# The HGRN head pipeline of a fused two-block layer, written out in another instruction order

## The chip, the cores and the metric

One core of a Trainium2 chip runs the whole kernel: TensorE (PE), VectorE (DVE), ScalarE (ACT), GpSimd (POOL) and SyncE (SP), which issues the loads. The metric is the device time of one execution, in microseconds. A head, below, is one of the eight heads of the HGRN recurrence.

## The reference, cut to what matters

The kernel computes two transformer-like blocks on 512 tokens of width 1024 with a context of 256 tokens. The change concerns one branch of the first block, the HGRN2 recurrence in both directions over 8 heads of 128 x 128, with the context scanned first:

```python
def _hgrn_gates(f_pre, lb):
    logf = jnp.log(lb + (1.0 - lb) * jax.nn.sigmoid(fp))
    k = (1.0 - lb) * jax.nn.sigmoid(-fp)

def body(S, inp):                       # _hgrn_scan, one chunk
    qc, kc, vc, lf = inp
    b = jnp.cumsum(lf, axis=2)
    decay = jnp.exp(jnp.where(mask, diff, -jnp.inf))
    attn = jnp.einsum('bhtd,bhtsd,bhsd->bhts', qc, decay, kc)
    o = jnp.einsum('bhtd,bhdv->bhtv', qc * jnp.exp(b), S) + jnp.einsum('bhts,bhsv->bhtv', attn, vc)
    S_new = jnp.exp(b_last)[..., None] * S + jnp.einsum(...)
    return S_new, o

hcf, s_f = scan_fn(*ctx_fwd, init)      # _bidir_scan: context, then latent, both directions
hlf, _ = scan_fn(*lat_fwd, s_f)
hcb, s_b = scan_fn(*_flip_t(ctx_bwd), init)
hlb, _ = scan_fn(*_flip_t(lat_bwd), s_b)
return hcf + jnp.flip(hcb, axis=2), hlf + jnp.flip(hlb, axis=2)
```

q is `silu` of a projection, f and k come from one projection for each direction, and v from another. All are float32.

## The kernel before, in words

Features lie on the 128 partitions and tokens along the free side. Every weight block is loaded by SP into `wraw` (3 buffers) and split into a rounded part `whi` on ACT (L203) and a remainder `wlo` on DVE (L204); `mm3` then multiplies `whi` by the two parts of the input (L215, L216) and `wlo` by the first (L218). A projection of 512 tokens is 24 such matmuls.

The recurrence is done without a scan over chunks: blocks of 8 tokens get running products of the gates (`hgrn_gates`, DVE, with two small ACT copies, L854 and L859 for direction 0, L865 and L870 for direction 1), block products are doubled level by level up to 128 tokens (`hgrn_blocks`, L898 and L913), and the attention matrix is put together from products at five sizes: `hgrn_level` makes `QM` on DVE and `KM` on POOL (L953, L956) and multiplies them into the PSUM banks X and Z (L961); the products inside a block of 8 go to Y1 and Y2 (L997). ACT copies X to `at` (L1035), DVE merges Z, Y1 and Y2 in with masks (L1036 to L1039), POOL adds the diagonal (L1040). `hgrn_ctx` makes the decays E of the context (DVE L882, L887, L890; POOL L891); E and the decayed keys `KL` (L1007) are transposed on PE (L1017, L1021), copied to `kt` by ACT (L1018, L1022) and multiplied with v into the state products `pk` (L1048, L1050). The states `st` start with an ACT copy (L1052) and go on in six DVE updates (L1063). The output is three matmuls for each 128 tokens (L1068 to L1070), read by ACT (L1075, L1076).

`hgrn_pipe` runs this as a software pipeline: in round h it finishes head h and prepares head n = h + 1 (projections, gates, block products, q). It stands in `tc.manual_schedule` (in `block1_hgrn`) for PE, DVE, ACT and POOL: these four engines issue the stage's instructions in the order in which the code writes them, and instructions of the next stage may be put between them. The loads of SP are placed by the planner. Buffers that set waits: PSUM `a` 4 banks (X, Z, Y1, Y2 and both `pk`), `p` 2 (all projections), `t` 2 (transposes and output); in SBUF `whi`, `wlo`, `wraw` 3 each and `w2` 17, which holds F, K, the q sigmoid, q, Q1, QM, KM, QL, KL, `at` and `st`.

In the order before, round h writes: gate projection 0 with its F and K sigmoids; q; levels 3 and 2; Y1, Y2; gate projection 1 with its sigmoids; levels 1 and 0; QL, KL; gates 0; all transposes with their `kt` copies; both context projections; the first weight split of head n + 1; gates 1; the `at` copy and the masks; block products; state products; both context decays; q projection; second weight split; state updates; output products; third split.

Of the kernel before, what the change touches and what calls it, by code (L numbers as in the profile page):

```python
# [8 lines left out]
F32 = mybir.dt.float32  # L9
F32R = mybir.dt.float32r  # L10
# [132 lines left out]
class Net:  # L143
# [668 lines left out]
    def hgrn_fx(self, h, d, wt):  # L812

        nc = self.nc
        j, c = (self.HFF, self.HFB)[d] + h, d * 8 + h
        ps = self.proj(wt, "x")
        F, K = self.w2("F"), self.w2("K")
        for t, b, sc in ((F, self.v("b_mix"), 1.0), (K, self.nbm, -1.0)):
            nc.scalar.activation(t.rearrange("p w r -> p r w"), ps.rearrange("p (r w) -> p r w", r=8), AF.Sigmoid,
                                 bias=b[:, j : j + 1], scale=sc)  # L820
            if t is F:
                nc.scalar.activation(F, F, AF.Identity, scale=self.omlb[:, c : c + 1], bias=self.lb[:, c : c + 1])
        return F, K

# [10 lines left out]

    def hgrn_gates(self, h, d, F, K, PS0):

# [15 lines left out]
        if d == 0:  # L853
            nc.scalar.activation(at(k_ + 2, q_ + 4), f(3, 4), AF.Copy)  # L854
            mu(at(k_ + 1, q_ + 5), f(2, 4), f(3, 5))
            mu(at(k_ + 0, q_ + 6), at(k_ + 1, q_ + 5), f(1, 6))
            mu(one(q_ + 7), one(q_ + 6), f(7))
            mu(PS0[:, 0, d], one(k_ + 0), f(0))
            nc.scalar.activation(PS0[:, 1, d], one(q_ + 7), AF.Copy)  # L859
            nc.vector.reciprocal(at(q_ + 0, k_ + 7), at(k_ + 0, q_ + 7))  # L860
            mu(at(q_ + 1, k_ + 6), at(q_ + 0, k_ + 7), f(1, 7))
            mu(at(q_ + 2, k_ + 5), at(q_ + 1, k_ + 6), f(2, 6))
            mu(one(k_ + 4), one(k_ + 5), f(5))
        else:
            nc.scalar.activation(at(q_ + 3, k_ + 5), f(3, 4), AF.Copy)  # L865
            mu(at(q_ + 2, k_ + 6), f(2, 4), f(3, 5))
# [8 lines left out]
        K1 = hx[:, 4 + 2 * (h % 2) + d].rearrange("p (b e) -> p b e", e=8)  # L875
        nc.gpsimd.tensor_tensor(K1, K, C[:, 1].rearrange("p (b e) -> p b e", e=8), ALU.mult)
        return K1

# [41 lines left out]
    def hgrn_q(self, h, ps):  # L920

        nc = self.nc
        bq = self.v("b_mix")[:, self.HQ + h : self.HQ + h + 1]
        sg, q = self.w2("sg"), self.w2("q")
        p8 = ps.rearrange("p (r w) -> p r w", r=8)
        nc.scalar.activation(sg.rearrange("p w r -> p r w"), p8, AF.Sigmoid, bias=bq)
        return sg, q, bq, p8

    def hgrn_q1(self, h, sg, q, bq, p8):
        nc = self.nc  # L930
        pm = lambda t: t.rearrange("p w r -> p r w")
# [9 lines left out]

    def hgrn_level(self, lv, dst, hb, Q1, K1, lev):

# [5 lines left out]
        for (o, a, p, i, e) in ((QM, Q1[0], pv(0, 0), 1, nc.vector), (QM, Q1[1], pv(1, 1), 0, nc.vector),  # L949
# [7 lines left out]
        qm, km = QM.rearrange("p b e -> p (b e)"), KM.rearrange("p b e -> p (b e)")  # L957
        for c in range(4):
            for b in range(128 // hb):
                bs = slice(c * 128 + b * hb, c * 128 + b * hb + hb)  # L960
                nc.tensor.matmul(dst[b * hb : b * hb + hb, bs], km[:, bs], qm[:, bs], start=True, stop=True)  # L961

    def hgrn_pipe(self, v):
# [9 lines left out]
        raw = self.hgrn_w(0)  # L973
        wt = [self.hgrn_split(r) for r in raw]
        PS0, K1, E = ps0(), [], []
        for d in range(2):
            K1.append(self.hgrn_gates(0, d, *self.hgrn_fx(0, d, wt[d]), PS0))
# [5 lines left out]
        wt = [self.hgrn_split(r) for r in raw]  # L983
        for h in range(8):
            n = h + 1
            more = n < 8
            if more:
                fx = [self.hgrn_fx(n, 0, wt[0])]
                PS0, K1n = ps0(), []
            Q1 = self.hgrn_q1(h, *pq)  # L990
            X, Z, Y1, Y2 = [self.bank("a") for _ in range(4)]
            self.hgrn_level(3, X, 128, Q1, K1, lev)
            self.hgrn_level(2, X, 64, Q1, K1, lev)
            for Y, d in ((Y1, 0), (Y2, 1)):
                for c in range(4):
# [14 lines left out]
            if more:  # L1010
                K1n.append(self.hgrn_gates(n, 0, *fx[0], PS0))
            kts = []
            for d in range(2):
                kt = w.tile([128, 5, 128], F32, tag="w5", bufs=2, name=self.nm("kt"))
                pt = self.bank("t")
                for i in range(2):
                    nc.tensor.transpose(pt[:, i * 128 : i * 128 + 128], E[d][:, i * 128 : i * 128 + 128], self.ident)  # L1017
                nc.scalar.activation(kt[:, 0:2], pt[:, :256].rearrange("p (c t) -> p c t", c=2), AF.Copy)  # L1018
                pt = self.bank("t")
                for i, c in enumerate(orders[d]):  # L1020
                    nc.tensor.transpose(pt[:, i * 128 : i * 128 + 128], KE[d][:, c * 128 : c * 128 + 128], self.ident)  # L1021
                nc.scalar.activation(kt[:, 2:5], pt[:, :384].rearrange("p (c t) -> p c t", c=3), AF.Copy)  # L1022
                kts.append(kt)
# [12 lines left out]
            nc.vector.copy_predicated(v4(at), m4(self.m8), v4(Z))  # L1036
# [28 lines left out]
            po = self.bank("o", [128, 4, 128])  # L1065
            for c in range(4):
# [1114 lines left out]
```

## Time and profile before

| | us |
|---|---|
| median of 3 runs | 2699.94 (2699.52 to 2700.64) |
| profiled execution, device time | 2698.25 |
| its span | 2696.5 |
| the HGRN heads, first to last output products | about 775 to 1103 |
| PE busy over the span | 2540.4 (94%) |
| DVE, ACT, POOL busy | 1592.2 (59%), 997.0 (37%), 461.4 (17%) |

How to read it: the span is the stretch between the first and the last instruction of one profiled execution; shares over all of it mix stages with different limits, so the rows further below are cut to single heads. In a timeline a row gives its start, how long it lasted, the engine, the line and what it wrote and read; neighbours of one kind are merged (`x4`), and a bracket tells how long the engine was idle before it and which instruction's end released it.

### The profile page before, as it was taken

The numbers are of one execution on the slowest core, as the hardware profiler recorded it, in microseconds if no ns is written. First come the engines' busy times: TensorE is split into PE (matmuls) and PEld (weight loads), VectorE is DVE, ScalarE is ACT, GpSimd is POOL, SyncE is SP. The second block draws the span as 40 slices with busy tenths as digits, with TensorE's granted clock in tenths as the row PEclk, the third lists the DMA queues.
The fourth block names the chain that finished last, engine by engine and source line by source line (L and its number), as shares of the span: only waits on it lengthen the run. The fifth ranks groups of instructions, "written<-read, shape, count | busy, mean of one in ns | idle before, by whom it ended". The sixth has DMA issues, their size and how long they took to land. (4 is left out here: it accounts for less than half of the span.)

```text
span 2696.5 us, 37860 instructions
## 1 busy us (share of the span) xinstructions
PE 2540.4 (94%) x15116; PEld 2177.0 (81%) x15116; DVE 1592.2 (59%) x2855; ACT 997.0 (37%) x1760; POOL 461.4 (17%) x539
## 2 busy tenths in 40 slices
PE   6999999999977877999999999999999998999998
PEld 4888888898866766889888898888886667988887
DVE  8777767746546546433543365666564676666665
ACT  6312212235333333242532244232343466533333
POOL 3000000021223323421400011034012351100001
PEclk8999999999988888999999999999999998999999
DMA  6535556512100101111133343344414223323332
GB/s 224 179 111 186 211 188 220 203 39 95 59 24 32 40 24 40 57 29 53 55 123 96 94 128 100 94 137 155 130 63 145 57 64 96 110 93 99 100 99 71
DMA packets 88305, 277.92 MB, mean 103 GB/s; under 512 B 12912, under 2 KB 31104, under 8 KB 79936
## 3 DMA queue, kind: packets, MB, share of 16 engines
q1 hardware_dynamic: 85344, 265.00, 30.4%
q0 software_dynamic: 2064, 7.35, 0.8%
q10 hardware_dynamic: 720, 3.15, 0.3%
q8 instruction: 119, 1.95, 0.3%
q14 instruction: 58, 0.48, 0.1%
HBM read 262.88 MB, written 12.59 MB: 102 GB/s over the span
## 5 line engine op out<-in xcount | busy, mean ns | idle before, releaser
L204 DVE TENSOR_TENSOR wlo<-wraw,whi 128x1024 fp32r<-128x1024 f32 (+1 forms) x341 | 424.9, 1252 | 288.5 <-ACT whi L203 159.4
L203 ACT ACTIVATE whi<-wraw 128x1024 fp32r<-128x1024 f32 (+1 forms) x341 | 354.1, 1052 | 492.3 <-PE psa L216 157.8
L215 PE MATMUL psp<-xmh,whi 128*128 128x512 f32 (+1 forms) x760 | 280.6, 378 | 3.2 <-ACT whi L203 2.1
L216 PE MATMUL psp<-xml,whi 128*128 128x512 f32 (+1 forms) x744 | 270.8, 372 | 0.0
L350 POOL TENSOR_TENSOR ssum<-ssum,sq 128x256 f32<-128x256 f32 x40 | 30.2, 755 | 962.0 <-ACT sq L348 961.7
L215 PE MATMUL psa<-xmh,whi 128*128 128x512 f32 x496 | 193.8, 391 | 0.0
L216 PE MATMUL psa<-xml,whi 128*128 128x512 f32 x496 | 193.7, 390 | 0.0
L215 PE MATMUL psu<-xmh,whi 128*128 128x512 f32 x496 | 193.5, 390 | 0.0
L216 PE MATMUL psu<-xml,whi 128*128 128x512 f32 x496 | 193.3, 390 | 0.0
L215 PE MATMUL pso<-hh,whi 128*128 128x512 f32 (+1 forms) x512 | 183.5, 364 | 3.4 <-DVE hr L496 3.4
L216 PE MATMUL pso<-hl,whi 128*128 128x512 f32 (+1 forms) x512 | 183.5, 364 | 0.0
L305 DVE SCALAR_TENSOR_TENSOR ajunk<-araw,crow 128x1024 bf16<-128x1024 f32 x128 | 156.2, 1221 | 26.1 <-DMA araw<-in_ada_r_dram 19.1
L215 PEld LDWEIGHTS psp<-xmh,whi 128*128 128x128 f32 x760 | 147.4, 194 | 28.7 <-ACT whi L203 2.6
L218 PE MATMUL psp<-xmh,wlo 128*128 128x512 f32 (+1 forms) x744 | 170.1, 368 | 0.0
L216 PEld LDWEIGHTS psp<-xml,whi 128*128 128x128 f32 x744 | 143.6, 193 | 23.0 <-issue 0.6
L492 DVE SCALAR_TENSOR_TENSOR xr<-pso,hgate,xr 128x512 f32<-128x512 f32 x128 | 95.2, 748 | 107.8 <-PE pso L218 107.6
L218 PEld LDWEIGHTS psp<-xmh,wlo 128*128 128x128 f32 x744 | 129.3, 189 | 26.1 <-issue 4.4
L218 PE MATMUL pso<-hh,wlo 128*128 128x512 f32 (+1 forms) x512 | 144.5, 363 | 0.0
L218 PE MATMUL psa<-xmh,wlo 128*128 128x512 f32 x496 | 126.8, 389 | 0.0
L218 PE MATMUL psu<-xmh,wlo 128*128 128x512 f32 x496 | 124.0, 390 | 0.0
L215 PEld LDWEIGHTS pso<-hh,whi 128*128 128x128 f32 x512 | 96.7, 189 | 18.0 <-DVE hr L496 3.6
L444 ACT ACTIVATE hh<-sa 128x512 fp32r<-128x512 f32 x66 | 36.7, 560 | 197.3 <-DVE sa L441 197.3
(661 smaller groups left out, 5804.6 us busy)
## 6 DMA issues: line engine op xcount, KB each, us to landing
araw<-in_ada_r_dram SPq DMA_DIRECT2D x52, 1024.0 KB, 5.3
wraw<-in_ffn_in_dram SPq DMA_DIRECT2D x88, 512.0 KB, 4.2
wraw<-in_mix_fm_dram SPq DMA_DIRECT2D x65, 512.0 KB, 3.6
wraw<-in_ffn_out_dram SPq DMA_DIRECT2D x44, 512.0 KB, 3.7
wraw<-in_up_dram SPq DMA_DIRECT2D x44, 512.0 KB, 3.7
wraw<-in_down_dram SPq DMA_DIRECT2D x22, 512.0 KB, 3.7
araw<-in_ada_w_dram SPq DMA_DIRECT2D x8, 1024.0 KB, 11.7
wraw<-in_mix_out_dram SPq DMA_DIRECT2D x14, 512.0 KB, 3.7
```

The costliest lines, as they stand in the source:

```text
L203: nc.scalar.activation(hi, raw, AF.Copy)
L204: nc.vector.tensor_tensor(lo, raw, hi.bitcast(F32), ALU.subtract)
L215: self.nc.tensor.matmul(ps, wh, xh, start=k == 0, stop=False)
L216: self.nc.tensor.matmul(ps, *((wl, xh) if last else (wh, xl)), start=False, stop=False)
L218: self.nc.tensor.matmul(ps, *((wh, xl) if last else (wl, xh)), start=False, stop=k == n - 1)
L305: nc.vector.scalar_tensor_tensor(junk, w[:, h], 1.0, cr[:, n], ALU.mult, ALU.mult, accum_out=o[:, k : k + 1])
L350: (eng or nc.vector).tensor_tensor(acc, acc, t, ALU.add)
L444: nc.scalar.activation(hh, sa, AF.Copy)
L492: self.anchor = nc.vector.scalar_tensor_tensor(res[n], p, gt[:, n : n + 1], res[n], ALU.mult, ALU.add)
```

## The change

The same instructions are written in another order, and four helpers are cut in two so that their parts can stand apart: the weight split (`hgrn_hi` on ACT, `hgrn_lo` on DVE), the gate sigmoids (F in `hgrn_fx`, K in `hgrn_kx`), the gates (`hgrn_gates` becomes a generator that stops behind its first ACT copy, with K1 in `hgrn_k1`) and the levels (`hgrn_level` for the elementwise part, `hgrn_products` for the matmuls). The transposes of one direction with their copies become `hgrn_turn`. q is written over its own sigmoid, so one `w2` buffer less is taken.

Round h now writes: q of head h; gate projection 0, F, the copy L854, K; levels 3 and 2 with their products; Y1, Y2; the elementwise part of levels 1 and 0; QL, KL; the remainder of the q weights of head n; the rest of gates 0 and K1; both context decays of head h; gate projection 1, F, the copy L865; the products of levels 1 and 0; the `at` copy; the transposes and copies of direction 0; the rest of gates 1, K, K1; context projection 0; the transposes and copies of direction 1; the loads of head n + 1 and the first `whi`; the masks; context projection 1; the first `wlo`; the state products; the second `whi`; block products; state updates; the second `wlo`; q projection; the third `whi`; output products. Ahead of the loop the first weight split of head 1 goes before the q projection of head 0. The diff, cut to its core (line numbers of the old file):

```diff
@@ -802 +802 @@
-    def hgrn_split(self, raw):
-        h, l = self.split_w(raw, [KT, 128])
+    def hgrn_hi(self, raw):
+        t = [self.wp.tile([128, KT, 128], F32R, tag="w" + i, name=self.nm("w" + i)) for i in ("hi", "lo")]
+        self.nc.scalar.activation(t[0], raw, AF.Copy)
+        return t, raw
+
+    def hgrn_lo(self, x):
+        (h, l), raw = x
+        self.nc.vector.tensor_tensor(l, raw, h.bitcast(F32), ALU.subtract)
         return [(h[:, k], l[:, k]) for k in range(KT)]
...
@@ -852 +863 @@ def hgrn_gates
             nc.scalar.activation(at(k_ + 2, q_ + 4), f(3, 4), AF.Copy)
+            yield
             mu(at(k_ + 1, q_ + 5), f(2, 4), f(3, 5))
...
@@ -921 +937 @@ def hgrn_q, hgrn_q1
-        sg, q = self.w2("sg"), self.w2("q")
+        sg = self.w2("sg")
...
-        nc = self.nc
+        nc, q = self.nc, sg
...
@@ -970 +999 @@ def hgrn_pipe
         fc = [self.hgrn_fc(0, d, wt[d]) for d in range(2)]
+        raw = self.hgrn_w(1)
+        wt[0] = self.hgrn_lo(self.hgrn_hi(raw[0]))
         pq = self.hgrn_q(0, self.proj(wt[2], "x"))
         lev, ends = self.hgrn_blocks(PS0)
-        E = [self.hgrn_ctx(0, d, *fc[d]) for d in range(2)]
-        raw = self.hgrn_w(1)
-        wt = [self.hgrn_split(r) for r in raw]
+        wt[1] = self.hgrn_lo(self.hgrn_hi(raw[1]))
+        wq = self.hgrn_hi(raw[2])
         for h in range(8):
             n = h + 1
-            more = n < 8
+            more, last = n < 8, n >= 7
+            Q1 = self.hgrn_q1(h, *pq)
             if more:
-                fx = [self.hgrn_fx(n, 0, wt[0])]
                 PS0, K1n = ps0(), []
-            Q1 = self.hgrn_q1(h, *pq)
+                F, ps = self.hgrn_fx(n, 0, wt[0])
+                gates = self.hgrn_gates(n, 0, F, PS0)
+                next(gates)
+                K = self.hgrn_kx(n, 0, ps)
             X, Z, Y1, Y2 = [self.bank("a") for _ in range(4)]
-            self.hgrn_level(3, X, 128, Q1, K1, lev)
-            self.hgrn_level(2, X, 64, Q1, K1, lev)
+            for lv, hb in ((3, 128), (2, 64)):
+                self.hgrn_products(X, hb, *self.hgrn_level(lv, Q1, K1, lev))
...
-            if more:
-                fx.append(self.hgrn_fx(n, 1, wt[1]))
-            self.hgrn_level(1, X, 32, Q1, K1, lev)
-            self.hgrn_level(0, Z, 128, Q1, K1, lev)
+            low = [(X, 32, *self.hgrn_level(1, Q1, K1, lev)), (Z, 128, *self.hgrn_level(0, Q1, K1, lev))]
...
             if more:
-                K1n.append(self.hgrn_gates(n, 0, *fx[0], PS0))
...
+                wt[2] = self.hgrn_lo(wq)
+                next(gates)
+                K1n.append(self.hgrn_k1(n, 0, K))
+            E = [self.hgrn_ctx(h, d, *fc[d]) for d in range(2)]
             if more:
-                fc = [self.hgrn_fc(n, d, wt[d]) for d in range(2)]
-                wq = wt[2]
-            if n < 7:
+                F, ps = self.hgrn_fx(n, 1, wt[1])
+                gates = self.hgrn_gates(n, 1, F, PS0)
+                next(gates)
+            for x in low:
+                self.hgrn_products(*x)
+            at = flat(self.w2("at"))
+            nc.scalar.activation(at, X, AF.Copy)
+            kts = [self.hgrn_turn(E[0], KE[0], orders[0])]
+            if more:
+                next(gates)
+                K = self.hgrn_kx(n, 1, ps)
+                K1n.append(self.hgrn_k1(n, 1, K))
+                fc = [self.hgrn_fc(n, 0, wt[0])]
+            kts.append(self.hgrn_turn(E[1], KE[1], orders[1]))
+            if not last:
                 raw = self.hgrn_w(n + 1)
-                wt = [self.hgrn_split(raw[0])]
-            if more:
-                K1n.append(self.hgrn_gates(n, 1, *fx[1], PS0))
-            at = flat(self.w2("at"))
+                hi = self.hgrn_hi(raw[0])
...
-            nc.scalar.activation(at, X, AF.Copy)
             nc.vector.copy_predicated(v4(at), m4(self.m8), v4(Z))
...
             nc.gpsimd.tensor_tensor(at, at, self.dg, ALU.add)
-            T128 = ends
             if more:
-                lev, ends = self.hgrn_blocks(PS0)
+                fc.append(self.hgrn_fc(n, 1, wt[1]))
+            if not last:
+                wt[0] = self.hgrn_lo(hi)
             pks, S = [], []
...
+            if not last:
+                hi = self.hgrn_hi(raw[1])
+            T128 = ends
             if more:
-                E = [self.hgrn_ctx(n, d, *fc[d]) for d in range(2)]
-                pq = self.hgrn_q(n, self.proj(wq, "x"))
-            if n < 7:
-                wt.append(self.hgrn_split(raw[1]))
+                lev, ends = self.hgrn_blocks(PS0)
             for i in range(3):
...
+            if not last:
+                wt[1] = self.hgrn_lo(hi)
+            if more:
+                pq = self.hgrn_q(n, self.proj(wt[2], "x"))
+            if not last:
+                wq = self.hgrn_hi(raw[2])
             po = self.bank("o", [128, 4, 128])
...
-            if n < 7:
-                wt.append(self.hgrn_split(raw[2]))
```

## Rows read from the trace of the kernel before

**Rows 1.** The page's first line, span of the profiled execution.

```profile
span 2696.5 us, 37860 instructions
```

**Rows 2.** Windows: us, busy PE, PEld, DVE, ACT, POOL; PEclk, DMA, GB/s.

```profile
877.31:928.45 51.14, 38.82 (x254) 34.32 (x254) 26.65 (x60) 17.24 (x34) 16.42 (x18) 0.87 0.10 30
...
1110.00:1300.00 190.00, 188.67 (x1311) 164.37 (x1309) 65.55 (x157) 69.47 (x219) 51.28 (x69) 1.00 0.14 44
```

**Rows 3.** Timeline, PE, head 3: start us, us, instruction, [idle before <-releaser].

```profile
887.97 1.67 PE L961 MATMUL psa<-QM,KM 128*128 128x128 f32 x24
889.57 2.05 PE L997 MATMUL psa<-Q,hgx 128*128 128x128 f32 x16
891.38 0.48 PE L215 MATMUL psp<-xmh,whi 128*128 128x512 f32 x1
...
897.01 1.55 PE L961 MATMUL psa<-QM,KM 128*32 128x32 f32 x40
...
901.84 0.44 PE L1017 MATMUL pst<-ident,E 128*128 128x128 f32 x2 [2.74 <-ACT kt L1018]
...
902.58 0.36 PE L215 MATMUL psp<-xmh,whi 128*128 128x256 f32 x1
...
913.64 1.22 PE L1048 MATMUL psa<-v,kt 128*128 128x128 f32 x4 [5.06 <-ACT at L1035]
...
917.81 0.48 PE L215 MATMUL psp<-xmh,whi 128*128 128x512 f32 x1
...
923.35 0.39 PE L1068 MATMUL pso<-v,at 128*128 128x128 f32 x2
...
928.45 0.80 PE L1070 MATMUL pso<-st,QL 128*128 128x128 f32 x2 [4.49 <-DVE st L1063]
```

**Rows 4.** Timeline, PE, head 6.

```profile
1065.04 1.22 PE L1048 MATMUL psa<-v,kt 128*128 128x128 f32 x4 [2.89 <-ACT at L1035]
```

**Rows 5.** Timeline, ACT, head 3.

```profile
897.12 1.18 ACT L819 ACTIVATE F<-psp,vec 128x512 f32<-128x512 f32 x1 [5.76 <-PE psp L218]
898.33 0.81 ACT L822 ACTIVATE F<-F,lbc,omlb 128x512 f32<-128x512 f32 x1
...
900.00 0.43 ACT L854 ACTIVATE hgx<-F 128x128 f32<-128x128 f32 x1
...
901.42 0.37 ACT L1018 ACTIVATE kt<-pst 128x256 f32<-128x256 f32 x1
...
913.00 0.58 ACT L1035 ACTIVATE at<-psa 128x512 f32<-128x512 f32 x1
...
923.55 1.19 ACT L926 ACTIVATE sg<-psp,vec 128x512 f32<-128x512 f32 x1 [5.19 <-PE psp L218]
```

**Rows 6.** Timeline, DVE, head 3.

```profile
878.38 1.17 DVE L932 SCALAR_TENSOR_TENSOR q<-psp,vec,sg 128x512 f32<-128x512 f32 x1
...
883.59 1.28 DVE L1006 TENSOR_TENSOR QL<-Q,ps 128x512 f32<-128x512 f32 x2
...
912.05 0.70 DVE L852 TENSOR_TENSOR hgx<-hgx,F 128x128 f32<-128x128 f32 x2
...
915.17 0.72 DVE L1036 COPY_PREDICATED at<-m,psa 128x512 f32<-128x512 int32 x1
...
917.94 0.28 DVE L898 TENSOR_TENSOR tots<-ps 128x128 f32<-128x128 f32 x1
...
921.72 0.41 DVE L882 TENSOR_SCALAR fc<-fc,omlb,lbc 128x256 f32<-128x256 f32 x1
...
925.62 1.23 DVE L204 TENSOR_TENSOR wlo<-wraw,whi 128x1024 fp32r<-128x1024 f32 x1 [1.33 <-ACT whi L203]
926.76 1.63 DVE L1063 SCALAR_TENSOR_TENSOR st<-st,tots,psa 128x128 f32<-128x128 f32 x6
```

**Rows 7.** Timeline, POOL, head 3.

```profile
881.66 4.33 POOL L956 TENSOR_TENSOR KM<-hgx,ps 128x256 f32<-128x256 f32 x2 [4.29 <-DVE QM L956]
```

**Rows 8.** Timeline, DVE, head 7.

```profile
1081.55 5.23 DVE L956 TENSOR_TENSOR QM<-Q,ps 128x256 f32<-128x256 f32 x6
```

More of the change, by code (lines that the diff above doesn't have):

```diff
@@ L814, in hgrn_fx, with hgrn_sig, hgrn_kx @@
         nc = self.nc
-        j, c = (self.HFF, self.HFB)[d] + h, d * 8 + h
+        c = d * 8 + h
         ps = self.proj(wt, "x")
[L817 to L823, printed above, removed]
+        F = self.hgrn_sig(h, d, ps, self.v("b_mix"), 1.0)
+        nc.scalar.activation(F, F, AF.Identity, scale=self.omlb[:, c : c + 1], bias=self.lb[:, c : c + 1])
+        return F, ps
+    def hgrn_sig(self, h, d, ps, b, sc):
+        t, j = self.w2("F"), (self.HFF, self.HFB)[d] + h
+        self.nc.scalar.activation(t.rearrange("p w r -> p r w"), ps.rearrange("p (r w) -> p r w", r=8), AF.Sigmoid,
+                                  bias=b[:, j : j + 1], scale=sc)
+        return t
+    def hgrn_kx(self, h, d, ps):
+        return self.hgrn_sig(h, d, ps, self.nbm, -1.0)
     def hgrn_fc(self, h, d, wt):
@@ L834, in hgrn_fc, with hgrn_gates @@
         return out
-    def hgrn_gates(self, h, d, F, K, PS0):
+    def hgrn_gates(self, h, d, F, PS0):
         nc, hx = self.nc, self.hgx
@@ L865, in hgrn_gates @@
             nc.scalar.activation(at(q_ + 3, k_ + 5), f(3, 4), AF.Copy)
+            yield
             mu(at(q_ + 2, k_ + 6), f(2, 4), f(3, 5))
@@ L874, in hgrn_gates, with hgrn_k1 @@
             mu(one(k_ + 3), one(k_ + 2), f(2))
-        K1 = hx[:, 4 + 2 * (h % 2) + d].rearrange("p (b e) -> p b e", e=8)
-        nc.gpsimd.tensor_tensor(K1, K, C[:, 1].rearrange("p (b e) -> p b e", e=8), ALU.mult)
+        yield
+    def hgrn_k1(self, h, d, K):
+        K1 = self.hgx[:, 4 + 2 * (h % 2) + d].rearrange("p (b e) -> p b e", e=8)
+        self.nc.gpsimd.tensor_tensor(K1, K, self.hgx[:, 2 * d + 1].rearrange("p (b e) -> p b e", e=8), ALU.mult)
         return K1
@@ L940, in hgrn_q1, with hgrn_level @@
         return out
-    def hgrn_level(self, lv, dst, hb, Q1, K1, lev):
+    def hgrn_level(self, lv, Q1, K1, lev):
         nc = self.nc
@@ L956, in hgrn_level, with hgrn_products @@
                 e.tensor_tensor(bv(o)[:, :, i], bv(a)[:, :, i], x.unsqueeze(3).broadcast_to([128, 32 // m, m, 8]), ALU.mult)
-        qm, km = QM.rearrange("p b e -> p (b e)"), KM.rearrange("p b e -> p (b e)")
+        return QM.rearrange("p b e -> p (b e)"), KM.rearrange("p b e -> p (b e)")
+    def hgrn_products(self, dst, hb, qm, km):
         for c in range(4):
@@ L960, in hgrn_level, with hgrn_turn @@
                 bs = slice(c * 128 + b * hb, c * 128 + b * hb + hb)
-                nc.tensor.matmul(dst[b * hb : b * hb + hb, bs], km[:, bs], qm[:, bs], start=True, stop=True)
+                self.nc.tensor.matmul(dst[b * hb : b * hb + hb, bs], km[:, bs], qm[:, bs], start=True, stop=True)
+    def hgrn_turn(self, E, KE, order):
+        nc = self.nc
+        kt = self.wk.tile([128, 5, 128], F32, tag="w5", bufs=2, name=self.nm("kt"))
+        for n, src, cs in ((0, E, (0, 1)), (2, KE, order)):
+            pt = self.bank("t")
+            for i, c in enumerate(cs):
+                nc.tensor.transpose(pt[:, i * 128 : i * 128 + 128], src[:, c * 128 : c * 128 + 128], self.ident)
+            nc.scalar.activation(kt[:, n : n + len(cs)], pt[:, : 128 * len(cs)].rearrange("p (c t) -> p c t", c=len(cs)), AF.Copy)
+        return kt
     def hgrn_pipe(self, v):
@@ L972, in hgrn_pipe @@
                 nc.gpsimd.memset(self.hgx[:, 2 * d + i].rearrange("p (b e) -> p b e", e=8)[:, :, e : e + 1], 1.0)
-        raw = self.hgrn_w(0)
-        wt = [self.hgrn_split(r) for r in raw]
-        PS0, K1, E = ps0(), [], []
+        wt = [self.hgrn_lo(self.hgrn_hi(r)) for r in self.hgrn_w(0)]
+        PS0, K1 = ps0(), []
         for d in range(2):
-            K1.append(self.hgrn_gates(0, d, *self.hgrn_fx(0, d, wt[d]), PS0))
+            F, ps = self.hgrn_fx(0, d, wt[d])
+            K = self.hgrn_kx(0, d, ps)
+            for _ in self.hgrn_gates(0, d, F, PS0):
+                pass
+            K1.append(self.hgrn_k1(0, d, K))
         fc = [self.hgrn_fc(0, d, wt[d]) for d in range(2)]
+        raw = self.hgrn_w(1)
+        wt[0] = self.hgrn_lo(self.hgrn_hi(raw[0]))
         pq = self.hgrn_q(0, self.proj(wt[2], "x"))
         lev, ends = self.hgrn_blocks(PS0)
-        E = [self.hgrn_ctx(0, d, *fc[d]) for d in range(2)]
-        raw = self.hgrn_w(1)
-        wt = [self.hgrn_split(r) for r in raw]
+        wt[1] = self.hgrn_lo(self.hgrn_hi(raw[1]))
+        wq = self.hgrn_hi(raw[2])
         for h in range(8):
             n = h + 1
-            more = n < 8
+            more, last = n < 8, n >= 7
+            Q1 = self.hgrn_q1(h, *pq)
             if more:
-                fx = [self.hgrn_fx(n, 0, wt[0])]
                 PS0, K1n = ps0(), []
-            Q1 = self.hgrn_q1(h, *pq)
+                F, ps = self.hgrn_fx(n, 0, wt[0])
+                gates = self.hgrn_gates(n, 0, F, PS0)
+                next(gates)
+                K = self.hgrn_kx(n, 0, ps)
             X, Z, Y1, Y2 = [self.bank("a") for _ in range(4)]
-            self.hgrn_level(3, X, 128, Q1, K1, lev)
-            self.hgrn_level(2, X, 64, Q1, K1, lev)
+            for lv, hb in ((3, 128), (2, 64)):
+                self.hgrn_products(X, hb, *self.hgrn_level(lv, Q1, K1, lev))
             for Y, d in ((Y1, 0), (Y2, 1)):
@@ L1010, in hgrn_pipe @@
             if more:
-                K1n.append(self.hgrn_gates(n, 0, *fx[0], PS0))
[L1012 to L1023, printed above, removed]
-            if more:
-                fc = [self.hgrn_fc(n, d, wt[d]) for d in range(2)]
-                wq = wt[2]
-            if n < 7:
+                wt[2] = self.hgrn_lo(wq)
+                next(gates)
+                K1n.append(self.hgrn_k1(n, 0, K))
+            E = [self.hgrn_ctx(h, d, *fc[d]) for d in range(2)]
+            if more:
+                F, ps = self.hgrn_fx(n, 1, wt[1])
[13 more added lines that the diff above has]
+            if not last:
                 raw = self.hgrn_w(n + 1)
-                wt = [self.hgrn_split(raw[0])]
-            if more:
-                K1n.append(self.hgrn_gates(n, 1, *fx[1], PS0))
-            at = flat(self.w2("at"))
+                hi = self.hgrn_hi(raw[0])
             m4 = lambda m: m.unsqueeze(1).broadcast_to([128, 4, 128])
             v4 = lambda t: t.rearrange("p (c t) -> p c t", c=4)
-            nc.scalar.activation(at, X, AF.Copy)
             nc.vector.copy_predicated(v4(at), m4(self.m8), v4(Z))
```

4 lines of the change are left out of this document (2 added, 2 removed).

## The prediction

> **What bounds the kernel now.** The change touches one stage only, the HGRN recurrence, so I first cut the span into stages with the windows view. From one head's output products to the next head's takes 51.14 us, and in it TensorE (PE) is busy 38.82 us at a mean granted clock of 0.87; right after the stage, from 1110 to 1300 us, it is busy 188.67 of 190 us at a clock of 1.00 [rows 2]. Nothing else is near full inside a head: VectorE 26.65 us, ScalarE 17.24, GpSimd 16.42. So the stage is bound by a ring of waits, and what follows it is bound by PE and takes over whatever time the stage gives back.
>
> Second I read PE's own timeline of head 3 for its waits. There are three: 2.74 us before the second set of transposes, for a `kt` copy of ScalarE; 5.06 us before the state products, for the `at` copy of ScalarE; 4.49 us before the output products, for VectorE's state update `st` [rows 3]. Together 12.29 us. Heads 0 to 5 repeat these three; head 6 has the first and 2.89 us of the second, and not the third [rows 4], since projections of the next stage fill in there; head 7 has little.
>
> Third, the same timeline shows the clock. The state products behind the 5.06 us wait, 20 instructions, take 913.64 to 917.81, 4.17 us, while 16 instructions of the same shape on `Q,hgx` take 1.81 us (889.57 to 891.38), 0.113 each [rows 3]: 1.2 against 2.4 GHz. After the 2.74 us wait nothing slows. So a long wait is paid a second time behind it.
>
> PE's work for one head at full clock, by starts in rows 3: X and Y products 3.41 (887.97 to 891.38), the two gate projections 5.63 each (891.38 to 897.01), low-level products and first transposes 2.09 (897.01 to 901.84 less 2.74), second transposes 0.74, two context projections 6.00 (902.58 to 913.64 less 5.06), q projection 5.54, state products 20 x 0.113 = 2.26, output products 24 x 0.113 = 2.71. Sum 34.0 us. The head's 51.14 is then 34.0 of work, 12.29 of waits, and 4.84 of low clock (1.91 of it on the state products).
>
> **The change, part by part.** No arithmetic instruction is added or dropped; the same ones stand in another order on the four written-out queues. I measure time from T, the end of the projection for the next head's backward gates (897.01 in rows 3).
>
> *First wait.* In the kernel before, `kt` stands on ScalarE behind both sigmoids of d=1 and the gate copy L854 of d=0, which starts at 900.00; `kt` runs at 901.42 though the transposes ended at 899.10 [rows 3, 5]. L854 held VectorE's gates up too. In the change L854 comes right behind F of d=0, before the second projection; `at` and the first `kt` come right behind L865. PE goes from the first transposes to a context projection, whose bank was freed long before, so `kt` has 3.0 us of cover. The wait goes.
>
> *Second wait.* The `at` copy ran at 913.00, behind the weight copies and all gate work of d=1 [rows 5]. Now its turn is at T + 2.56: F starts with the end of the projection (897.12), its scaling ends at 899.14, which is T + 2.13, and L865 takes 0.43 [rows 5]. PE wants the bank at T + 2.09 + 3.0 + 0.74 + 3.0 = T + 8.8. The wait goes with its low clock. The second state bank is Z's and needs VectorE's first mask copy, below.
>
> *Third wait.* S waited at 926.76 for the block products (917.94 to 921.72), the context decays from 921.72 and a weight remainder at 925.62 [rows 6]. Now the decays stand before F of d=1 and the second remainder after S. VectorE's new run from T: second gate product at T + 2.56; gates 3.12 (912.05 to 915.17) plus at most 0.8, because L870 now stands behind `at` (0.58) and two `kt` copies (0.37 and at most 0.58) where it would be wanted 0.70 in: T + 6.5. Masks 2.77 (915.17 to 917.94): T + 9.3. Weight remainder 1.23: T + 10.5. Blocks 3.78: T + 14.3. S 1.63: T + 15.9 [rows 5, 6]. PE reaches the output products at T + 8.8 + 2.26 + 5.54 = T + 16.6. So S is 0.7 us early: this is the tightest place of the new order, and the wait goes only just.
>
> *Closing the ring.* The q sigmoid runs T + 16.6 to 17.8 (1.19). q to QL takes 6.49 on VectorE when GpSimd is not in the way (878.38 to 884.87): T + 24.3; the moved remainder of the q weights 1.23: T + 25.5 [rows 5, 6]. PE has outputs until 19.3 and the next gate projection until 25.0, F is ready at 27.1, L854 at 27.5. Gates until 31.2 (0.5 more for L859, which waits behind the K sigmoid), decays at most 3.9 (921.72 to 925.62): T + 35.1. The next d=1 gates can start at 34.0 + 2.56 = T + 36.6. So VectorE is free 1.5 us early and the ring closes on PE's 34.0.
>
> *New waits on in-order queues.* L859 on ScalarE waits for VectorE's gates with F of d=1 queued behind it; it is due near T + 28.5, F at T + 34.0. L870 has the K sigmoid of d=1 behind it, and the second context projection needs the bank which that sigmoid frees: sigmoid done at about T + 5.6, PE there at T + 5.8. Covered by 0.2 us; if VectorE starts these gates x late, PE loses about x here. On GpSimd the K1 product of d=0 now stands ahead of the decay products; the first is wanted by the transposes at T + 35.4 and ready by about T + 33.3. The three weight loads of SP move behind the second transposes; two of their buffers are free a whole head early, the third by the moved remainder at T + 25.5 with some 26 us until ScalarE wants it. The hi copies run after `kt`, after `st` and after the q sigmoid, each behind the last reader of its buffer. I put all of these at nothing. Writing q over its sigmoid and taking K's buffer later frees buffers of the 17; no row prices that: between nothing and one wait of 2.74 us per head as a gain; I take nothing, since PE no longer waits there.
>
> *Contention.* VectorE and GpSimd slow each other in this trace: two `KM` products lasted 4.33 us and had waited 4.29 while VectorE ran its products [rows 7], and in head 7, with both engines in the run, six `QM` products lasted 5.23 us [rows 8]. The new order puts GpSimd's `KM` and `KL` beside q to QL in every head. Its price there is between nothing and 5.23 us; against 1.5 us of room plus the 0.7 before S, PE would lose at most 3.0 us per head and likely none to 1. I take 0.5, and keep 3.0 for the range. The Trainium skill, page "SBUF — State Buffer", section "Who interferes with whom", says that a VectorE instruction with two SBUF inputs and a GpSimd instruction that reads SBUF exclude one another for the whole instruction, and that masks and updates reading PSUM stay out of it. Rows 7 agree that one waits for the other; taken to its end it is the second rival below.
>
> *Sum.* A head takes 34.0 + 0.5 = 34.5. Heads 0 to 5 save 51.14 - 34.5 = 16.64 each, 99.8. Head 6 saves 2.74 + 2.89 + 1.91 - 0.5 = 7.0. Start and end of the pipe (weights and decays reordered once each, next-stage projections filled in by the planner) have no row of their own; I take nothing and allow one wait, 5.06 us, either way. 106.9 off the profiled execution's 2698.25 (its span of 2696.5 and 1.75 around it [rows 1]) is 2591.4; the median lies 1.69 above that execution: **2593**.
>
> **The rivals.**
> 1. *VectorE becomes the bound through GpSimd.* It is late by 1.7 us at the d=1 gates (5.23 of delay less rooms), and once more in gates and decays beside K1 and the decay products. A head takes about 37, saving 6 x 14.1 + 5 = 90: 2610. For it: rows 7 and 8; against: much of the delay falls into VectorE's waits for F.
> 2. *The two engines exclude each other throughout.* Then a head cannot be shorter than 26.65 + 16.42 = 43.1 us [rows 2]: saving 48 + 4, 2648. Against: those busy times already hold waiting on each other, as in the 4.33 us of two products [rows 7].
> 3. *The third wait stays.* S has 0.7 us of room; if the run from T to S is some 5 us longer than its rows, PE waits about 4.49 again and pays the 2.93 of low clock behind it: a head of 41.4, saving 58 + 7, 2635.
> 4. *The ring is not opened.* A wait that I have not seen (a slot, a bank) replaces the three, and a head stays near 51: no change.
> 5. *Slower: PE's clock stays low.* If short waits are spread through the head and the clock stays at 1.2 GHz behind each, the 34.0 of work costs up to 34.0 more. It decides once more than half of a head's matmul work is at 1.2 GHz (17.1 us extra); at two thirds a head takes 56.7 and the kernel about 2733. Against: behind 2.74 us nothing fell, and behind 5.06 us full clock was back by 917.81 [rows 3].
>
> **How the numbers follow.** Forecast (heads of 34 to 35.5 us, 2580 to 2606 with the ends): 0.60. Rival 1: 0.17, rival 2: 0.06, rival 3: 0.09, rival 4: 0.03, rival 5: 0.05. The forecast, rival 1 and all of rival 3 but its upper part make about 0.83, so the range is 2578 to 2638. A measurement of this kernel tells about 0.2% (5.4 us) from no change. Faster takes the forecast and rivals 1 to 3 with a small part of 4: 0.93; same 0.02; slower 0.05.
>
> **What would show it.** After: PE's waits on `at` and `kt` gone from its list of waits; a head of 34 to 35 us between output products; clock 0.97 or more in it; state products 0.113 us apart; VectorE over 70% busy; L859 and L870 waiting little. A wait of PE on `st` is rival 3, on the K sigmoid or `QM` rival 1, QM products of 0.8 us and more everywhere rival 2. The prediction is wrong if heads take over 38 us, or if the stage shrinks and the total does not, because the planner orders the next stage worse.

## The result, and the profile after

The changed kernel takes 2575.89 us (median of 4 runs, 2572.53 to 2581.02) against 2700.29: a ratio of 0.954, 95% interval 0.952 to 0.956. Forecast were 2593 in 2578 to 2638: the direction and the mechanism hold, and the time lies 2 us below the range, less than the runs of this kernel differ among themselves. The profiled execution takes 2574.22 us, 124.0 less than that of before.

The first matmul on `hh` of the stage after the recurrences starts at 1181.8 us and not at 1300.4: 118.6 us earlier. The first gate sigmoid of the HGRN stage, ahead of which nothing is reordered, starts 2.1 us later than before; so the stage itself, counted from that sigmoid, takes 477.4 us and not 598.1, which is 120.7 less. The other 5.4 come behind it and are dealt with in the first experiment. Before, then after:

```profile
702.32 1.23 ACT L819 ACTIVATE F<-psp,vec 128x512 f32<-128x512 f32 x1 [2.22 <-PE psp L218]
...
1300.39 0.60 PE L1348 MATMUL pst<-ident,hh 128*128 128x128 f32 x4
```

```profile
704.42 1.23 ACT L829 ACTIVATE F<-psp,vec 128x512 f32<-128x512 f32 x1 [2.22 <-PE psp L218]
...
1181.77 0.60 PE L1385 MATMUL pst<-ident,hh 128*128 128x128 f32 x4
```

| end of a head's output products to the next, us | heads 1 to 5 | head 6 | head 7 |
|---|---|---|---|
| before | 51.1 to 51.2 | 45.1 | 23.0 |
| after | 33.36 to 33.39 | 35.9 | 21.4 |

One head of after in the windows view (us; busy PE, PEld, DVE, ACT, POOL; granted clock, DMA share, GB/s), the answer to [rows 2]:

```profile
860.66:894.02 33.36, 33.36 (x257) 29.80 (x256) 31.21 (x60) 17.27 (x34) 15.44 (x18) 1.00 0.17 48
```

PE is busy from end to end at full clock, 33.36 us for work that kept it busy 38.82 us at a mean clock of 0.87 before. So of the 17.78 us that a head is shorter, 12.29 are its three waits and the other 5.5 are low clock and restarts behind them. VectorE has gone from 26.65 of 51.14 us to 31.21 of 33.36. The whole list of what PE waited for between 735 and 1000 us (total, times, longest) is short, and both entries are of the last head; and one wait stands ahead of the first head's products:

```profile
PE pso L1109 <- DVE st L1096: 1.3, 1, 1.3
PE pst L988 <- POOL E L905: 0.3, 1, 0.3
...
731.10 2.29 PE L979 MATMUL psa<-QM,KM 128*128 128x128 f32 x24 [3.92 <-DVE QM L972]
```

PE's timeline of one head, with the starts that [rows 3] has for before (gate projection d=1, low-level products, first context projection, second transposes, second context projection, state products, q projection, output products, the product that needs S, next gate projection):

```profile
836.25 0.48 PE L215 MATMUL psp<-xmh,whi 128*128 128x512 f32 x1
...
841.88 1.55 PE L979 MATMUL psa<-QM,KM 128*32 128x32 f32 x40
...
843.73 0.36 PE L215 MATMUL psp<-xmh,whi 128*128 128x256 f32 x1
...
846.69 0.38 PE L988 MATMUL pst<-ident,E 128*128 128x128 f32 x2
...
847.15 0.37 PE L215 MATMUL psp<-xmh,whi 128*128 128x256 f32 x1
...
850.10 0.60 PE L1081 MATMUL psa<-v,kt 128*128 128x128 f32 x4
...
852.25 0.47 PE L215 MATMUL psp<-xmh,whi 128*128 128x512 f32 x1
...
857.82 0.39 PE L1107 MATMUL pso<-v,at 128*128 128x128 f32 x2
...
858.41 0.49 PE L1109 MATMUL pso<-st,QL 128*128 128x128 f32 x2
...
860.66 0.48 PE L215 MATMUL psp<-xmh,whi 128*128 128x512 f32 x1
```

State products now take 2.15 us (850.10 to 852.25; 4.17 before). T, the end of the d=1 projection, is 841.88. VectorE's timeline of the same head (QM products; first gate product of d=0; of d=1; the last two block steps; state updates; second weight remainder):

```profile
829.42 3.88 DVE L972 TENSOR_TENSOR QM<-Q,ps 128x256 f32<-128x256 f32 x6
...
836.23 0.39 DVE L863 TENSOR_TENSOR hgx<-F 128x128 f32<-128x128 f32 x1
...
844.08 0.51 DVE L863 TENSOR_TENSOR hgx<-F 128x128 f32<-128x128 f32 x1 [0.63 <-ACT F L824]
...
855.62 0.66 DVE L929 COPY ps<-ps 128x128 f32<-128x128 f32 x1
856.20 0.61 DVE L914 TENSOR_TENSOR tots<-tots 128x8 f32<-128x8 f32 x1
856.73 1.63 DVE L1096 SCALAR_TENSOR_TENSOR st<-st,tots,psa 128x128 f32<-128x128 f32 x6
858.28 1.37 DVE L812 TENSOR_TENSOR wlo<-wraw,whi 128x1024 fp32r<-128x1024 f32 x1
```

S ends at 858.36 (T + 16.5) and the product that needs it starts at 858.41: VectorE arrives just when PE does.

### The profile page after: what moved, and what is told of

Read it like the earlier page. It is cut to its first block, busy times and chain, and to the rows that moved or that the text cites. A ratio compares the mean times of both kernels' runs of the same rounds, so it can differ in the third digit from the quotient of the medians.

```text
span 2572.4 us, 37867 instructions
## 1 busy us (share of the span) xinstructions
PE 2499.2 (97%) x15116; PEld 2141.9 (83%) x15116; DVE 1616.0 (63%) x2855; ACT 997.1 (39%) x1760; POOL 454.0 (18%) x539
## 5 line engine op out<-in xcount | busy, mean ns | idle before, releaser
L204 DVE TENSOR_TENSOR wlo<-wraw,whi 128x1024 fp32r<-128x1024 f32 (+1 forms) x317 | 391.5, 1240 | 230.6 <-ACT whi L203 102.9
L203 ACT ACTIVATE whi<-wraw 128x1024 fp32r<-128x1024 f32 (+1 forms) x317 | 330.0, 1052 | 473.0 <-PE psa L216 144.6
L215 PE MATMUL psp<-xmh,whi 128*128 128x512 f32 (+1 forms) x760 | 275.4, 371 | 1.1 <-ACT F L829 0.5
L218 PE MATMUL psu<-xmh,wlo 128*128 128x512 f32 x496 | 124.0, 390 | 0.0
```

The lines of the kernel that those rows point to most:

```text
L203: nc.scalar.activation(hi, raw, AF.Copy)
L204: nc.vector.tensor_tensor(lo, raw, hi.bitcast(F32), ALU.subtract)
L215: self.nc.tensor.matmul(ps, wh, xh, start=k == 0, stop=False)
L218: self.nc.tensor.matmul(ps, *((wh, xl) if last else (wl, xh)), start=False, stop=k == n - 1)
```

## The experiments

**The same kernel again.** No edit.

> The changed kernel itself once more. Of the 124.0 us between the two profiled executions, 118.7 lie in the HGRN stage and 5.5 in the attention stage of the second block, where next to nothing was reordered. Theory: those 5.5 us are the clock of one execution and not the change; then the head of 33.36 us comes back to 0.1 us, and the attention stage comes out somewhere between 474 and 480 us. Rival: the change causes them; then the stage takes 474 us again. Time 2572 to 2581.

2578.21 us (2574.17 to 2580.16); heads of 33.35 to 33.40 us. The attention stretch, from the last `s5b` transpose to the last `P` transpose, took 432.3 us in this profile, 431.6 in the first of after and 436.7 in that of before. That alone leaves the rival standing. But over the other kernels of this study it took 438.0, 431.8, 432.2, 435.6 and 428.4 us with the HGRN order of before or parts of it, and 431.9, 436.5, 435.2, 432.8 and 432.3 with that of after: the two groups overlap, 428 to 438 and 432 to 437. (The expectation counts from the first such transpose, which adds 42.3 us: 474.6 here, where theory and rival meet.) So about 5 us is what one profile of this stretch differs from another, and the 5.4 us are no effect that can be laid to the change. The part ahead of the HGRN stage differs as much: over the 13 profiles its first gate sigmoid starts between 700.6 and 706.4 us, in no order with the change. The stage counted from that sigmoid comes back to 0.1 us, 477.5 against 477.4.

### Moves on the kernel before

**Only the `at` copy early.**

```diff
             self.hgrn_level(0, Z, 128, Q1, K1, lev)
+            at = flat(self.w2("at"))
+            nc.scalar.activation(at, X, AF.Copy)
```

(and its lines ahead of the masks gone)

> The kernel before with only the `at` copy moved, to just behind the low-level products, so that the first state bank is free long before PE wants it. Forecast's terms, each wait worth its own row: the second wait and its low clock go in heads 0 to 6, 5.06 + 1.91 us each, 46 us. Rival (a ring: VectorE's order sets the pace, the waits are where PE meets it): the wait only moves to the second state bank, which the first mask frees behind the d=1 gates, and the head stays near 51 us; saving 0 to 5 us.

2716.32 us, ratio 1.0065 (1.0049 to 1.0081): longer by 17 us, heads of 54.5 us. PE's timeline (second transposes, a context matmul, first state products, second state products):

```profile
912.96 0.44 PE L1019 MATMUL pst<-ident,E 128*128 128x128 f32 x2 [3.25 <-ACT kt L1020]
...
914.05 0.42 PE L216 MATMUL psp<-xml,whi 128*128 128x256 f32 x1
...
921.04 0.60 PE L1048 MATMUL psa<-v,kt 128*128 128x128 f32 x4
...
928.63 1.19 PE L1048 MATMUL psa<-v,kt 128*128 128x128 f32 x4 [6.32 <-DVE at L1036]
```

The wait on `at` has become a longer one on the first mask, as the ring says. The loss is the other two rows. The copy now stands ahead of `kt` and makes PE's first wait 3.25 us where it was 2.74, and behind it the clock falls, as it did not in the kernel before. (The length of the wait alone does not decide that, as the next two kernels show.) The windows view of 2 us each, this kernel and then the kernel before, each just behind that wait:

```profile
914.00:916.00 2.00, 2.00 (x12) 0.50 0.00 0
```

```profile
902.00:904.00 2.00, 1.97 (x17) 1.00 0.00 0
```

Context matmuls start 0.21 us apart for sixteen of them and not 0.12: 1.5 us more, and with the 0.5 the sigmoids, the weight copy, the gates of d=1 and the masks behind them are 2.0 us later. The rest of the 3.4 us lies in the q projection, which now runs its first eight matmuls at 1.2 GHz.

**Only S early.** The state updates go ahead of the block products and the decays.

```diff
             T128 = ends
-            if more:
-                lev, ends = self.hgrn_blocks(PS0)
@@ behind the state products
+            for i in range(3): ... the state updates ...
             if more:
+                lev, ends = self.hgrn_blocks(PS0)
                 E = [self.hgrn_ctx(n, d, *fc[d]) for d in range(2)]
```

> The kernel before with only the state updates S moved, ahead of the block products, the context decays and the second weight remainder. Forecast's terms: the third wait and its low clock go in heads 0 to 5, 4.49 + 2.93 us each, 44 us; heads near 43.7 us. Rival (a ring): the work put behind S delays the next head's q and QM products and a new wait stands there; saving under 20 us.

2694.22 us, ratio 0.9984 (0.9974 to 0.9994), heads of 51.2 us. The 4.49 us wait is gone from PE's timeline; in its place:

```profile
885.48 1.13 PE L961 MATMUL psa<-QM,KM 128*128 128x128 f32 x8 [1.91 <-DVE QM L956]
887.48 1.12 PE L961 MATMUL psa<-QM,KM 128*64 128x64 f32 x16 [0.87 <-DVE QM L956]
```

The waits shrink by 1.7 us in sum and PE's busy time grows from 38.82 to 40.59, at a clock of 0.83 against 0.87. The head is as long as before, but not by the ring alone: the `kt` wait is as long as in the kernel before, and this time the clock falls behind it, from 1.00 to 0.50 (in heads 1 to 6), so that the second transposes and context projections take 1.5 us more.

```profile
903.20 0.44 PE L1017 MATMUL pst<-ident,E 128*128 128x128 f32 x2 [2.73 <-ACT kt L1018]
```

```profile
904.00:906.00 2.00, 2.00 (x12) 0.50 0.00 0
```

**Both.**

> Both moves of the two kernels beside it. Forecast's terms add: 46 + 44, 90 us, heads near 36.7 us. Rival (a ring): not the sum; if the `at` copy alone gives nothing, this is the same as the early S alone.

2684.7 us, ratio 0.9941 (0.9925 to 0.9958), heads of 48.8 and 50.1 by turns. Neither the sum of the terms nor the early S alone: 15 us, where the single moves gave +17 and -5. PE still has 3.25 for `kt`, 6.33 for the first mask and 2.2 for QM. Behind the 3.25 us the clock stays at 1.00 in every second head and falls to 0.50 in the others; the row and the window of one where it stays:

```profile
899.34 0.44 PE L1019 MATMUL pst<-ident,E 128*128 128x128 f32 x2 [3.25 <-ACT kt L1020]
```

```profile
900.00:902.00 2.00, 2.00 (x19) 1.00 0.00 0
```

**Only the transposes and `kt` early.** They go, with their copies, ahead of `K1n.append(self.hgrn_gates(n, 0, *fx[0], PS0))`.

> The kernel before with only the transposes and their `kt` copies moved, ahead of the d=0 gates (L854), still behind the K sigmoid of d=1. Forecast's terms: the first wait shrinks from 2.74 us to about 1.4, 9 us over seven heads. Rival (a ring): what PE gains there it waits longer for the `at` copy, since that hangs on the weight copy and gates queued on ScalarE and VectorE; no change.

2685.59 us, ratio 0.995 (0.9936 to 0.9965). PE's timeline:

```profile
896.08 0.44 PE L1015 MATMUL pst<-ident,E 128*128 128x128 f32 x2 [1.37 <-ACT kt L1016]
907.87 1.22 PE L1048 MATMUL psa<-v,kt 128*128 128x128 f32 x4 [5.06 <-ACT at L1035]
```

The 1.37 us are gained in full and the 5.06 stay, so the first wait is a link of the ring: the weight copy and the gates of d=1 that lead to `at` come behind the context projections, and these behind the transposes. 13.7 us are somewhat more than 7 x 1.37 = 9.6; in its profile the stage is 10.9 us shorter. Heads are 48.8 and 50.4 by turns: PE is busy 37.86 us in the shorter and 38.99 in the longer, and idle for the rest; the mean clock is 0.88 in both.

**The early moves together.** Transposes and `kt`, then both directions' gates and the `at` copy, then the context projections; S ahead of the blocks. Weights, decays and K sigmoids stay.

```diff
-            if more:
-                K1n.append(self.hgrn_gates(n, 0, *fx[0], PS0))
             kts = []
             ... transposes and kt ...
+            if more:
+                K1n.append(self.hgrn_gates(n, 0, *fx[0], PS0))
+                K1n.append(self.hgrn_gates(n, 1, *fx[1], PS0))
+            at = flat(self.w2("at"))
+            nc.scalar.activation(at, X, AF.Copy)
             if more:
                 fc = [self.hgrn_fc(n, d, wt[d]) for d in range(2)]
```

> The kernel before with the early moves together and nothing else: transposes and `kt` copies ahead of the gates, both directions' gates and the `at` copy ahead of the context projections, the state updates S ahead of block products and decays. The weight steps, the context decays and the K sigmoids keep their places. Theory (the ring runs from the projection of d=1 over ScalarE's queue, where L865 and the gates of d=1 stand behind the context projections' sigmoids and the weight copy, to the masks and S): with the d=1 gates ahead of these the ring opens, S is ready when PE comes, and what stays is a wait for QM of 3 to 4 us, since blocks, decays and weight remainders now stand between S and q: heads of 38 to 42 us, 65 to 80 us off before. Rival (the ring hangs on the steps left in place): heads of 48 us and more, under 20 us off.

2656.46 us, ratio 0.9837 (0.9817 to 0.9857): 43 us off, heads of 44.3 to 44.8 (46.9 for head 1). Between the two expectations. PE's timeline:

```profile
886.28 0.44 PE L1015 MATMUL pst<-ident,E 128*128 128x128 f32 x2 [1.37 <-ACT kt L1016]
894.31 0.71 PE L1045 MATMUL psa<-v,kt 128*128 128x128 f32 x4 [1.30 <-ACT at L1026]
899.12 0.99 PE L1045 MATMUL psa<-v,kt 128*128 128x128 f32 x4 [3.43 <-DVE at L1035]
...
917.54 1.13 PE L961 MATMUL psa<-QM,KM 128*128 128x128 f32 x8 [1.82 <-DVE QM L956]
919.09 0.69 PE L961 MATMUL psa<-QM,KM 128*64 128x64 f32 x16 [0.42 <-DVE QM L956]
```

S is in time and the d=1 gates no longer hold `at` up, as the theory said; but the masks still wait behind the weight remainder on VectorE, which waits for a copy behind the context sigmoids, and blocks, decays and remainders still stand ahead of QM. So a third of the change's gain comes from these early moves. The other two thirds come with what else the change moves, the weight steps, decays and sigmoids above all; how they share it was not taken apart.

As the parts around the stage differ by some 5 us from profile to profile, here are the moves once more, by the median of the whole time and by the stage from the first gate sigmoid to the first matmul on `hh` (one profile each):

| change against the kernel before, us | whole time | stage |
|---|---|---|
| only the `at` copy early | +17.0 | +20.9 |
| only S early | -5.1 | -1.0 |
| both | -14.6 | -8.5 |
| only the transposes and `kt` early | -13.7 | -10.9 |
| the early moves together | -43.1 | -37.4 |
| the whole change | -124.4 | -120.7 |

### Moves on the changed kernel

**The second weight remainder ahead of S.**

```diff
+            if not last:
+                wt[1] = self.hgrn_lo(hi)
             for i in range(3):
```

> The changed kernel with one step moved: the second weight remainder stands before the state updates S and not behind them, 1.2 us more of VectorE ahead of S in heads 0 to 5. Theory (S arrives just when PE wants it, as the profile of after shows): all of it becomes a wait of PE, heads of 34.5 us, 7 us in all, no fall of the clock. Rival (the forecast's 0.7 us of room): 0.5 us per head, 3 us in all. Rival (PE has cover from elsewhere): nothing.

2583.66 us, heads of 34.5; PE's timeline:

```profile
900.12 0.49 PE L1109 MATMUL pso<-st,QL 128*128 128x128 f32 x2 [1.09 <-DVE st L1098]
```

1.1 us per head, what the remainder adds ahead of S (1.13 us from its start to that of S), paid in full at a clock of 1.00. S had no room.

**The decays before S.**

```diff
                 lev, ends = self.hgrn_blocks(PS0)
+                E = [self.hgrn_ctx(n, d, *fc[d]) for d in range(2)]
```

> The changed kernel with the context decays of the next head computed between the block products and S, as in the kernel before, and not ahead of the d=1 gates. VectorE has 2.6 to 3.4 us more before S in seven heads. Theory: PE waits about that long before the output products, heads of 36 to 36.8 us, 18 to 24 us in all, and the clock stays full, as it did behind the 2.74 us wait of before. Rival: the clock falls behind the wait as it did behind 4.49 us; then 2.9 us more per head, 38 to 44 us in all. Rival (the decays are not what delayed S): nothing.

2587.93 us, heads of 34.95: 1.6 us each and not 2.6 or more. PE's row, and VectorE's where the decays start and S starts:

```profile
900.44 0.49 PE L1110 MATMUL pso<-st,QL 128*128 128x128 f32 x2 [1.56 <-DVE st L1097]
```

```profile
896.28 0.41 DVE L898 TENSOR_SCALAR fc<-fc,omlb,lbc 128x256 f32<-128x256 f32 x1
...
898.78 1.61 DVE L1097 SCALAR_TENSOR_TENSOR st<-st,tots,psa 128x128 f32<-128x128 f32 x6
```

The decays take 2.5 us there (3.5 in after, 839.90 to 843.44, beside GpSimd's K1), and the last two block steps 0.2 us each where they took 0.6 in after with GpSimd's KM beside them. The theory was right that the wait comes and that the clock stays at 1.00 behind it; the size was not: what stands beside a step on GpSimd changes with its place.

**More work for VectorE.** Each QL product is written twice.

> The changed kernel with each QL product computed twice: 1.36 us more of VectorE per head in the run from q to QL, nothing else. Theory (VectorE is as good as full in the new order, idle 0.66 us per head): about 0.7 us per head goes to PE, heads of 34.1 us, 5 us in all. Rival (the forecast's 1.5 us of room there): heads of 33.4 us, no change. Rival (VectorE and GpSimd exclude each other and every addition is paid in full and more): 1.4 us and more per head, 10 us or more in all.

2584.13 us, heads of 34.25, 0.9 us each for 1.36 of added work. The wait stands at the first transposes, for the decays that come after the gates:

```profile
880.31 0.44 PE L988 MATMUL pst<-ident,E 128*128 128x128 f32 x2 [0.91 <-POOL E L905]
```

So VectorE had about 0.5 us of room in that part, not the 1.5 of the forecast.

**q in a buffer of its own.** `sg, q = self.w2("sg"), self.w2("q")`, as before.

> The changed kernel with q in a buffer of its own again, as before. Theory (the forecast's: the freed buffer is worth nothing, as PE does not wait for it): heads of 33.36 us, no change. Rival (the 17 buffers were part of the old waits): a wait for a buffer on GpSimd's KM or KL or on F, heads longer by 0.5 us and more.

2580.05 us (2578.2 to 2581.26), heads of 33.33 to 33.46 and no new wait of PE: the freed buffer is worth nothing here. The time does not stand apart from the 2578.21 of the kernel run again.

**The start of the pipe.** `wt[1] = self.hgrn_lo(hi)` moved, in head 0, behind the first QM products.

> The changed kernel with one step moved at the start of the pipe: the second weight remainder of head 1 stands behind the first QM products of head 0 and no longer ahead of q. PE waits 3.92 us there in the changed kernel. Theory (VectorE's queue ahead of q, 2.2 us of waiting for and computing that remainder, sets it): the wait falls to about 1.7 us, 2 to 4 us off the stage with the clock behind it, heads the same; in the whole time that is within the spread of the runs. Rival (the sigmoid or KM comes last): the wait stays over 3 us.

2574.31 us (2571.70 to 2575.31). PE's rows where the 3.92 us wait stood:

```profile
724.20 1.13 PE L979 MATMUL psa<-QM,KM 128*128 128x128 f32 x8 [0.86 <-DVE QM L972]
...
726.63 1.12 PE L979 MATMUL psa<-QM,KM 128*64 128x64 f32 x16 [1.30 <-DVE QM L972]
```

The wait falls to 2.16 us in two parts. Head 0's last output product starts at 755.1 us against 760.0 and 760.4, but most of that lies ahead of the stage, whose first gate sigmoid starts at 700.6 us here against 704.0 and 704.4. Counted from there 1.4 to 1.5 us are gained, at head 0 and at the end of the stage alike: not the 2 to 4 expected. In the whole time it is inside the spread of the runs, so it is the best version here by its trace and not by a measured ratio.

## Why the prediction was right or wrong

*What bounds the kernel.* Right: a ring, and behind it a stage that takes over the time given back (118.6 us at its first row). What the three waits are together was read right. How little a single move brings was not said in the forecast and is the study's main finding: single moves gave +17, -5 and -14 us, the early moves together -43, the whole order -124. That the waits are links of one ring is shown where a wait came back at the next link (the `at` copy early, S early); in both of these the clock takes its part of the loss.

*First and second wait.* Right: both are gone, and 20 state products take 2.15 us.

*Third wait.* Right in outcome, by the narrowest margin. S was forecast at T + 15.9 and PE at T + 16.6; S ends at T + 16.5 with PE there. The 0.7 us of room did not exist, and two misses offset each other, which is luck: the blocks took 4.76 us (851.97 to 856.73) and not 3.78, 0.9 of it in the last two steps, 0.66 and 0.61 beside GpSimd's KM where they took 0.22 and 0.16 before; the gates from their second product on took 3.34 and not the 3.9 allowed.

*Closing the ring.* Right that PE closes it. VectorE's room was forecast at 1.5 us and is 0.63 by its idle time (the wait at 844.08), about 0.5 by the added work. From the end of the scaling of F for d=0 (834.28 + 0.81) the gates start 1.1 us late, at 836.23: from q to QL VectorE took 8.95 us and not 6.49, 1.8 of the difference because six QM products took 3.88 us where they took 2.09 in head 3 of before.

```profile
880.91 2.09 DVE L956 TENSOR_TENSOR QM<-Q,ps 128x256 f32<-128x256 f32 x6
```

*Contention.* The allowance between 0 and 3.0 us held, and of the 0.5 that I took nothing was paid by PE. VectorE paid: the 60 instructions of a head keep it busy 31.21 us where it was 26.65, and its idle time took up the difference. Rival 1 (heads of 37) and rival 2 (43.1) did not come; VectorE and GpSimd together are busy 46.65 us in a head of 33.36, so the exclusion in the Trainium skill, page "SBUF — State Buffer", section "Who interferes with whom", taken over all their work, is not what this trace shows. On pairs of products that read SBUF alone it is visible: of after's six QM products the first two took 1.31 us each beside GpSimd's KL, and those behind them, with GpSimd idle, 0.41; in head 3 of before GpSimd's KM took 3.73 us while nine VectorE products ran at 0.41 to 0.68 us each. The first two rows are VectorE's in after, the third GpSimd's in before:

```profile
829.42 1.31 DVE L972 TENSOR_TENSOR QM<-Q,ps 128x256 f32<-128x256 f32 x1
```

```profile
831.88 0.41 DVE L972 TENSOR_TENSOR QM<-Q,ps 128x256 f32<-128x256 f32 x1
```

```profile
881.66 3.73 POOL L956 TENSOR_TENSOR KM<-hgx,ps 128x256 f32<-128x256 f32 x1 [4.29 <-DVE QM L956]
```

The 4.29 us ahead of it, which the forecast counts as slowing too, ended with a VectorE product and its semaphore; by the trace they are a wait on that product and not contention. Rivals 3, 4 and 5 did not come either.

*The sum, and the step that failed.* The mechanism held; the step that failed is the sum, where three terms saved too little. In numbers: 124.0 was found and 106.9 forecast, 17.1 apart.

1. A head, priced at 34.0 + 0.5 = 34.5, took 33.36: six times 1.14 is 6.8. Of the 1.14, 0.5 is the contention taken, which PE did not pay. The other 0.64 is PE's work: the starts of rows 3 carry pieces of restart (second transposes 0.74 there, 0.46 now; low-level products and first transposes 2.09 there, 1.85 now).
2. Head 6 was priced at 7.0, and the start and end of the pipe at nothing: 118.6 less 6 x 17.78 is 11.9, so 4.9 more. Head 6 gave 9.3, as the clock behind its wait was priced on the state products alone, and the low clock at its own start, behind head 5's third wait, at nothing (0.8 us each in the q projection and in the first gate projection). Head 7 gave 1.6. The start gave 3.2, less the 2.1 by which the first gate sigmoid came later.
3. What lies behind the stage was put at nothing and gave 5.4, the spread of the attention stretch.

No one of them put the time outside the range by itself. The sum at its floor (heads of 34.0, and one wait of 5.06 at the ends) gives about 2584.5; the low end of 2578 was 6.5 lower, without a row for it. The time went through it because PE's work was 0.64 shorter per head than that floor (3.9 us), the ends used nearly all of their 5.06, and the 5.4 came on top. The last of these is chance, and the margin is small: in the second set of runs of the same kernel the median is 2578.21, inside the range.

*Signs.* Of the signs named, waits gone (in heads 1 to 6), clock 1.00 and VectorE over 70% (94%) came; heads of 34 to 35 us were named and 33.36 came; state products are 0.1075 us apart, not 0.113.

## What to carry to other kernels

Where PE waits at several places of one loop and no engine is full, lay out the whole period for all queues, as one timetable, before moving anything: a wait taken out alone can come back at the next link, and longer (only the early `kt` kept its gain here). The period is the largest of PE's work at full clock and each ring through the queues; when the new order is near balance, work added ahead of the last link is paid in full (1.1 us for 1.13 here), so leave the engine that closes the ring some room. And give the range what single profiles of the untouched stages differ by, below as well as above.

## What the runs showed of the hardware

What a PE wait costs in clock cannot be read from its length. Before the second transposes of a head, a wait of 2.74 us left the clock at 1.00 (2.4 GHz) in the kernel before, and one of 2.73 us in the same place was followed by 0.50 (1.2 GHz) with only S early. A wait of 3.25 us there was followed by 0.50 with only the `at` copy early, which made sixteen context matmuls 1.5 us longer, and by 1.00 in every second head with both moves. What PE had done earlier in the head differs between these kernels; no run takes apart which of it decides.

VectorE and GpSimd delay each other on products of two SBUF operands: a QM product took 1.31 us beside GpSimd's KL and 0.41 with GpSimd idle, and a KM product of GpSimd 3.73 us beside VectorE's products and the next one, behind them, 0.65. So a VectorE step's price depends on its place: six QM products took 2.09 us in head 3 of before, 3.88 in the new order and 5.23 in [rows 8]; the decays 2.5 or 3.5 by where they stand.
